# L copied from PSUM ahead of the masked product, and a score factor moved into q's norm weights, in a two-layer diffusion trunk

## Chip, core and metric

The kernel runs on one core of a Trainium2 chip, as one program. The metric is the device time in microseconds (us), of which three runs are shown below; smaller is better.

## What is computed

Two layers of a hybrid trunk over 640 tokens (512 latent, 128 context) with 1024 features, in float32. The first layer pairs MLA attention with retention, the second pairs differential attention (4 heads, two score maps of 64 features each) with a bidirectional RWKV-7 scan (8 heads of 64). Each layer ends in a gated convolutional FFN. What the change touches lies in the second layer:

```python
# differential attention, scale = 64 ** -0.5 = 0.125
q = rms_norm(dq, qn); k = rms_norm(dk, kn)
s = einsum('bqhcd,bkhcd->bchqk', q, k) * scale
p = softmax(s); w = p[:, 0] - lam * p[:, 1]; o = w @ v
# RWKV-7, one token at a time
state = state * w_t - (state @ kk_t) (kk_t * a_t)^T + v_t k_t^T
y_t = state @ r_t
```

## The kernel before

**Stages.** The program runs layer 0, then the FFN, then the input products of layer 1 (`odd_in`, `rwkv_in`), then the scan (`rwkv`, about 1045 to 1505 us of the span), then the output products and the second FFN. In the scan two streams are woven by hand: the main stream is the RWKV scan, the side stream (`side_mix`) first makes the differential q, k and v (`odd_qkv`) and then runs the differential attention (`diff_attn`). `BG` says how many steps of the side stream go into each part of the scan, and matrix products of the side stream are issued behind a main product of `LAG` = 4 events before. The final order of each engine's queue is made by the framework's scheduler when the program is built, from a timeline of its own; on the chip each engine works through its queue in that order.

**The scan.** It works on five groups g, each a block of 128 tokens forward and one backward. For each group there are three jobs: `pre(g)` makes the matrices of a block, `lb` and `lc` solve a small triangular system from the matrix L, and `steps(g)` carries the state over the two half blocks. They are staggered: with `steps(g)` run `pre(g+2)` and `lb(g+1)`, `lc(g+1)`.

**L.** In `rw_pre`, for each direction and each half block q, eight products (lines 1858 and 1859) fill the PSUM banks `sa` and `sb`, one bank each; the pool that these banks come from has two buffers in the scan. Then for s = 0 (`sa`) and s = 1 (`sb`) four instructions follow: VectorE multiplies the bank by the mask `mk` into `st[s]` (line 1863, 128x512, tile `hq`), ScalarE copies the left half of the rows into `L` (line 1864), GpSimd copies the right half into `rb` (line 1865), and ScalarE puts `kr` into the rows of `st[s]` that are now free (line 1866). That is 40 pairs of `sa` or `sb` in all. When both directions are done, `rw_leaf_a` sends L to DRAM and back (`ld<-L`, `LI<-ld`, lines 1884 and 1887); `rw_leaf_b` solves with 31 pairs of VectorE operations (lines 1901 and 1902), which read L above the diagonal only; `xd` goes to DRAM and back; `rw_leaf_c` makes `X11h` on ScalarE (line 1929) and writes `zb`, which `steps` needs.

**The scores.** In `diff_attn`, `s1` runs 40 times (4 heads, 5 query tiles, 2 maps): products into the one score buffer `sc` (line 1442), a row maximum with the sign turned (line 1445, VectorE), that maximum times 0.125 (line 1446, VectorE), and the exponential with that bias and the factor 0.125 (line 1448, ScalarE, tile `p`), which frees `sc` for the next one.

**q's norm weights.** `odd_qkv` multiplies q by its 64 weights `dqn`, which lie in the constant tile `rt` (line 1288, GpSimd).

Of the kernel before, what the change touches and what calls it, by code (L numbers as in the profile page):

```python
# [13 lines left out]
OP = mybir.AluOpType  # L14
# [90 lines left out]
def _consts3():  # L105
    """Head sums land in rows 32 p + i; the selectors bring rows 32 p + i and 32 p + 2 + i back to half i of tile p."""
    out = np.zeros((128, C3LEN), np.float32)
    st = out[:, C3OFF["st64"][0]:]
    st[:64, 0] = 1.0
    st[64:, 1] = 1.0  # L110
    st[:, 32:34] = 1.0 / 128
    sel = out[:, C3OFF["sel"][0]:].reshape(128, 4, 2, 64)
    for p in range(4):
        for i in range(4):
            sel[32 * p + i, p, i % 2] = 1.0
    return out
# [92 lines left out]

"""How the streams of the layers are woven: background steps in each part of the scan, spans of layer 0."""  # L210
BG = (89, 24, 102, 0, 22, 72, 0)
# [5 lines left out]
class Side:  # L217
    """A background stream: its matrix products are issued behind the main streams' product of LAG events before."""

# [21 lines left out]
def weave(bg, rate, *parts):  # L241
    """Advance several emission streams together; each (generator, begin, end) spreads evenly over [begin, end]."""
    ev = []
    for i, (g, b, e) in enumerate(parts):
        n = NSTEP[g.__name__]
        for k in range(n):
            ev.append((b + (e - b) * k / n, i))
    ev.sort()
    for _, i in ev:
        n0 = len(bg.traced()) if bg is not None else 0  # L250
        next(parts[i][0], None)
        if bg is not None:
            bg.mark(n0)
            bg.acc += rate / len(ev)
            while bg.acc >= 1:
                bg.acc -= 1
                bg.step()
    for g, _, _ in parts:
        for _ in g:
            pass  # L260


class Trunk:
# [116 lines left out]
    def setup_late(self):  # L380
        """The loads that nothing needs before the first products."""
        nc, a = self.nc, self.a
        self.rt = self.cp.tile([128, RLEN], F32, name="rt")
        for t, src in ((self.rt, bass.AP(tensor=a["row"].tensor, offset=a["row"].offset, ap=[[0, 128], [1, RLEN]])), (self.ct, a["cst"])):
            i = nc.sync.dma_start(t, src)
            self.tc.add_manual_dep(i.ins, self.fetched.ins.name, mybir.DependencyInfo(mybir.DependencyClass.NoSync, mybir.DependencyReason.DATA),
                                   reason="later")
        self.sel = self.cp.tile([128, 4, 128], F32R, name="sel")
        sel = self.W("sel", 512)
        nc.sync.dma_start(sel, a["cst3"][:, 64:])  # L390
        nc.gpsimd.tensor_copy(self.sel.rearrange("p a f -> p (a f)"), sel)
# [164 lines left out]
    def ada_half(self, c0):  # L556
        """Eight chunks of layer 0's modulation, from pieces that the queue brings in this order."""
        nc = self.nc
# [29 lines left out]
    def norm_mod(self, side):  # L588
        """Layer 0: rstd and x * rstd do not wait for the modulation."""
        nc = self.nc  # L590
# [25 lines left out]
    def norm_begin(self, l, which, pool):  # L616
        """Open the next norm: every final x[k] is scaled by the modulation and split at once, its rstd is applied after the
        matrix product; two more columns carry the shifts through it."""
        nc = self.nc
# [18 lines left out]
    def norm_end(self, us, rb):  # L638
        """Close the norm: the first three products run while the rstd is being worked out."""
        nc = self.nc  # L640
# [16 lines left out]
    def fm_norm(self, h, u, rb, ps=None):  # L657
        """One output tile of the normalised product, into the padded columns of u."""
        nc = self.nc
# [103 lines left out]
    def head_sums(self, sqs, stat, mmt, tile):  # L763
        """Per-head sums of four tiles of squares: [tokens, (token tile, tile, half)]."""
        nc = self.nc
# [15 lines left out]
    def head_rows(self, r, mmt, tile):  # L781
        """The [tokens, (token tile, tile, half)] columns as rows of hi and lo parts."""
        nc = self.nc
# [15 lines left out]
    def head_bcast(self, rows, p, mmt):  # L799
        """Tile p of the rows, spread over the features of its two heads."""  # L800
        mm = mmt()
        for b, e in ((192, 512), (512, 832)):
            for i, r in enumerate(rows):
                self.nc.tensor.matmul(mm[:, b:e], self.sel[:, p], r[:, b - 192:e - 192], start=i == 0, stop=i == len(rows) - 1)
        return mm[:, 192:832]

# [1 line left out]
    def even_jobs(self):  # L808
# [126 lines left out]
    def mla_cached(self, kr, ccs, D):  # L935
        """Keys and values of the cache, before the first products."""
        nc, a = self.nc, self.a
# [38 lines left out]
    def mla_rows(self, src, dst, tt, g, gain, D, tr):  # L976
        """Four heads of 128 tokens, turned to rows of features."""
        nc = self.nc
# [281 lines left out]

# [1 line left out]
    def odd_jobs(self):  # L1262
# [3 lines left out]
    def odd_qkv(self, D):  # L1266
        """Differential q, k, v from the stored h: one 256-column group at a time, its post-processing one group behind."""
        nc, a = self.nc, self.a
        with self.pool("qk", 1, "left") as qp, self.psum("qps", 2) as qps, self.psum("qtr") as qtr:
            def tile(s, w, bufs, dt=F32):  # L1270
                return qp.tile([128, w], dt, name=self.nm(s), tag=s, bufs=bufs)

            rope = qp.tile([128, 2, 4, 64], F32, name="ropd")
            nc.scalar.dma_start(rope.rearrange("p a t d -> p (a t d)"), a["ropd"])
# [92 lines left out]
    def odd_out(self, D):  # L1367
        """The differential half of w_out covers the end of the RWKV half."""
        nc = self.nc
# [38 lines left out]
    def diff_attn(self, D, ap, scp, trp):  # L1408
        nc, a = self.nc, self.a
        nlam = self.diff_lam(ap)  # L1410
        scale = 64 ** -0.5

# [22 lines left out]
        def s1(q, k, qt, so):  # L1435
            n = 768 if qt < 4 else 128
            pr = []
            for c in range(2):
# [6 lines left out]
                nc.vector.tensor_reduce(mx, sc[:, :n], axis=AX.X, op=OP.max, negate=True)  # L1445
                nc.vector.tensor_scalar(mx, mx, scale, None, op0=OP.mult)
                p = ap.tile([128, 768], F32, name=self.nm("p"), tag="p", bufs=4)[:, :n]
                nc.scalar.activation(p, sc[:, :n], AF.Exp, bias=mx, scale=scale, accum_out=sm)
                pr.append((p, sm))
# [291 lines left out]
    def rwkv_out(self, D, rp, o):  # L1741
        """D["u"] holds gate * gain and gate * v."""
        nc = self.nc
# [42 lines left out]
    def rw_pre(self, F, f, d, tt, L, hs, ex):  # L1786
# [52 lines left out]
        for q in range(2):  # L1839
# [21 lines left out]
            for s, rw, ps in ((0, lo, sa), (1, hi, sb)):  # L1861
                yield
                nc.vector.tensor_tensor(st[s], ps.rearrange("p (a c) -> p a c", a=4), mk, op=OP.mult)
                nc.scalar.copy(L[rw, sl, :], st[s][rw, :, 0:64])
                nc.gpsimd.tensor_copy(rb[rw], st[s][rw, :, 64:128])
# [248 lines left out]
```

## Time and profile before

| | |
|---|---|
| device time, three runs | 2068.95, 2071.0, 2071.74 us (median 2071.0) |
| span of the profiled execution, first to last instruction | 2059.5 us |
| device time around the span, against the three runs | 9.5 to 12.2 us |
| PE busy in the span | 1952.7 us (95%) |
| DVE, ACT, POOL busy | 1253.8, 887.3, 186.5 us |

The profile is one execution; its own device time isn't listed beside its span, so the three runs stand for it. PE is TensorE's products, PEld its weight loads, DVE is VectorE, ACT ScalarE, POOL GpSimd, SPq the queue of SyncE that issues transfers. In a row `out<-in` names what an instruction writes and reads, `x40` how often; after it stand times in us or, for the mean of one, in ns. `<-X` names what ended an engine's idle time.

### The profile page before, as it was taken

How to read it: one execution, taken by the hardware profiler on the slowest of the kernel's cores; microseconds unless marked ns; L12 is line 12 of the kernel's file. 1: busy time of each engine (PE TensorE's matmuls, PEld its weight loads, DVE VectorE, ACT ScalarE, POOL GpSimd, SP SyncE). 2: the span in 40 equal slices, each digit the busy share in tenths (PEclk: the TensorE clock that was granted, in tenths of full speed). 3: DMA queues.
4: the chain of work that ended last, by engine and by line, in shares of the span. 5: the costliest groups of instructions: out<-in, count | busy, mean ns of one | idle time of the engine just before them, and what ended most of it. 6: DMA issues, size and time to landing. Idle time of an engine off the chain costs nothing.

```text
span 2059.5 us, 36275 instructions
## 1 busy us (share of the span) xinstructions
PE 1952.7 (95%) x14376; PEld 1765.7 (86%) x14376; DVE 1253.8 (61%) x2752; ACT 887.3 (43%) x1680; POOL 186.5 (9%) x365
## 2 busy tenths in 40 slices
PE   6999999999999999999989897898779999999999
PEld 3998565999899899999978676777679999999999
DVE  6554657556456465577436856877667764656555
ACT  4433344334244243456333334667534542524343
POOL 1001000000000000000024332332110000000000
PEclk9999999999999999999989998979989999999999
DMA  8237344234543512143264554454453212122221
GB/s 323 67 109 242 105 134 163 89 104 147 181 153 116 192 62 83 60 151 104 83 207 100 109 161 120 100 116 96 100 200 106 77 58 92 60 85 67 77 63 71
DMA packets 190676, 243.60 MB, mean 118 GB/s; under 512 B 90730, under 2 KB 132970, under 8 KB 190508
## 3 DMA queue, kind: packets, MB, share of 16 engines
q1 hardware_dynamic: 184880, 225.87, 35.7%
q0 software_dynamic: 3904, 13.37, 2.2%
q8 instruction: 113, 1.85, 0.4%
q10 hardware_dynamic: 1724, 2.06, 0.3%
q14 instruction: 55, 0.45, 0.1%
HBM read 202.05 MB, written 39.21 MB: 117 GB/s over the span
## 4 chain that ended last, share of the span: by engine, by line
PE 81%; DVE 7%; DMA 6%; ACT 3%; issue 2%; POOL 1%; SPq 0%; ACTq 0%; DVEq 0%; POOLq 0%
PE mm L470 59%; PE qkv L1325 2%; PE ada L541 2%; PE rv L913 1%; PE pv L1130 1%; PE mm L1097 1%; DMA dk<-pt 1%; PE ptr L1120 1%; PE sc L1442 1%; DVE X L1902 1%; DVE tmp L1901 1%; DMA xd<-X 1%; DMA mq<-tr 1%; DMA raw<-ada 1%; PE mm L1098 1%
## 5 line engine op out<-in xcount | busy, mean ns | idle before, releaser
L414 ACT CAST hi<-raw 128x1024 fp32r<-128x1024 f32 (+4 forms) x212 | 195.9, 925 | 574.1 <-PE mm L470 528.6
L470 PE MATMUL mm<-hhi,hi 128*128 128x322 f32 x1648 | 381.0, 312 | 0.0
L470 PE MATMUL mm<-hlo,hi 128*128 128x322 f32 x1648 | 380.3, 311 | 0.0
L470 PE MATMUL mm<-hhi,lo 128*128 128x322 f32 x1648 | 380.1, 311 | 0.0
L470 PEld LDWEIGHTS mm<-hhi,hi 128*128 128x128 f32 x1648 | 278.3, 189 | 8.7 <-issue 6.7
L470 PEld LDWEIGHTS mm<-hlo,hi 128*128 128x128 f32 x1648 | 279.5, 190 | 0.0
L470 PEld LDWEIGHTS mm<-hhi,lo 128*128 128x128 f32 x1648 | 278.6, 189 | 0.0
L415 DVE TENSOR_TENSOR lo<-raw,hi 128x1024 fp32r<-128x1024 f32 (+4 forms) x212 | 226.1, 1067 | 58.7 <-ACT hi L414 36.0
L672 DVE SCALAR_TENSOR_TENSOR x<-mm,ada,x 128x512 f32<-128x512 f32 (+1 forms) x176 | 88.7, 545 | 176.1 <-PE mm L470 175.9
L470 PE MATMUL mm<-ahi,hi 128*128 128x320 f32 x704 | 161.7, 311 | 0.0
L470 PE MATMUL mm<-ahi,lo 128*128 128x320 f32 x704 | 160.7, 309 | 0.0
L470 PE MATMUL mm<-alo,hi 128*128 128x320 f32 x704 | 160.3, 309 | 0.0
L663 DVE COPY shv<-mm 128x2 f32<-128x2 f32 x103 | 16.3, 159 | 207.9 <-PE mm L470 207.9
L470 PEld LDWEIGHTS mm<-ahi,hi 128*128 128x128 f32 x704 | 117.1, 188 | 12.0 <-ACT hi L414 10.1
L1325 PE MATMUL qkv<-w,x 128*128 128x256 f32 x480 | 118.9, 402 | 0.1
L470 PEld LDWEIGHTS mm<-ahi,lo 128*128 128x128 f32 x704 | 117.8, 188 | 0.0
L470 PEld LDWEIGHTS mm<-alo,hi 128*128 128x128 f32 x704 | 117.6, 188 | 0.0
L666 ACT ACTIVATE u<-u,shv 128x128 f32<-128x128 f32 (+1 forms) x176 | 90.3, 557 | 48.8 <-DVE u L665 47.0
L734 DVE SCALAR_TENSOR_TENSOR ac<-u,vt,ac 128x642 f32<-128x642 f32 x88 | 78.0, 887 | 52.5 <-ACT ac L732 52.3
L1325 PEld LDWEIGHTS qkv<-w,x 128*128 128x128 f32 x480 | 94.0, 201 | 17.0 <-issue 1.7
L732 ACT ACTIVATE ac<-u,vt 128x642 f32<-128x642 f32 x88 | 81.3, 925 | 2.8
L665 DVE TENSOR_TENSOR u<-mm,rb 128x128 f32<-128x128 f32 (+1 forms) x176 | 77.3, 481 | 2.5 <-ACT rb L650 2.5
(419 smaller groups left out, 3351.3 us busy)
## 6 DMA issues: line engine op xcount, KB each, us to landing
raw<-ada SPq DMA_DIRECT2D x96, 512.0 KB, 4.6
raw<-up SPq DMA_DIRECT2D x88, 512.0 KB, 3.5
raw<-down SPq DMA_DIRECT2D x32, 384.0 KB, 3.1
raw<-down SPq DMA_DIRECT2D x32, 320.0 KB, 2.8
fs<-df SPq DMA_DIRECT2D x10, 832.0 KB, 5.2
raw<-wb_fm SPq DMA_DIRECT2D x15, 512.0 KB, 3.5
w<-wb_tm SPq DMA_DIRECT2D x12, 512.0 KB, 4.5
raw<-wa_fm SPq DMA_DIRECT2D x11, 512.0 KB, 4.3
```

The lines of the kernel that those rows point to most:

```text
L414: nc.scalar.copy(hi, t)
L415: nc.vector.tensor_tensor(lo, t, hi.bitcast(F32), op=OP.subtract)
L470: nc.tensor.matmul(ps[:, c0 + b:c0 + e], wt[:, ws], at[:, b:e], start=first and j == 0, stop=last and j == 2)
L541: nc.tensor.matmul(ps[32 * j:32 * j + 32, :], self.cs[:, k, :], pieces[j // 2][:, (j % 2) * 512:(j % 2) * 512 + 512], start=k == 0, stop=k ...
L665: nc.vector.tensor_tensor(u[:, o], ps[:, s], rb[:, s], op=OP.mult)
L666: nc.scalar.activation(u[:, o], u[:, o], AF.Identity, bias=sh[:, c:c + 1])
L672: nc.vector.scalar_tensor_tensor(x[:, s], ps[:, s], self.ada_v(l, part, m, c), x[:, s], op0=OP.mult, op1=OP.add)
L732: nc.scalar.activation(ac, u[:, 1:643], AF.Identity, scale=cv[:, 1, f:f + 1], bias=self.vec(f"cb{l}", f))
L734: nc.vector.scalar_tensor_tensor(ac, u[:, 0:642], cv[:, 0, f:f + 1], ac, op0=OP.mult, op1=OP.add)
L913: nc.tensor.matmul(ps[:, :272], at[:, ts], wt[:, k * 272:k * 272 + 272], start=n == 0, stop=n == 23)
L1097: nc.tensor.matmul(sc[:, 0:512], q, kT[:, 0:4], start=True, stop=True)
L1325: nc.tensor.matmul(ps, h[k][:, t * 128:t * 128 + 128], w[k // 4][:, k % 4 * 256:k % 4 * 256 + 256], start=k == 0, stop=k == 7)
```

## The change

`L` is copied from the PSUM bank itself, and this copy now stands ahead of the masked product in the program; the masked product reads the same bank after it. The mask is no longer applied to L, of which only the part above the diagonal is read. The factor 0.125 is multiplied once into the 64 weights `dqn` at the start of `odd_qkv`; the 40 multiplications of the maximum and the factor in the exponential are gone. The rest of the diff takes away comments.

```diff
@@ odd_qkv
+            nc.vector.tensor_scalar(self.row("dqn"), self.row("dqn"), 0.125, None, op0=OP.mult)
             rope = qp.tile([128, 2, 4, 64], F32, name="ropd")
@@ diff_attn
         nlam = self.diff_lam(ap)
-        scale = 64 ** -0.5
...
                 nc.vector.tensor_reduce(mx, sc[:, :n], axis=AX.X, op=OP.max, negate=True)
-                nc.vector.tensor_scalar(mx, mx, scale, None, op0=OP.mult)
                 p = ap.tile([128, 768], F32, name=self.nm("p"), tag="p", bufs=4)[:, :n]
-                nc.scalar.activation(p, sc[:, :n], AF.Exp, bias=mx, scale=scale, accum_out=sm)
+                nc.scalar.activation(p, sc[:, :n], AF.Exp, bias=mx, accum_out=sm)
@@ rw_pre
             for s, rw, ps in ((0, lo, sa), (1, hi, sb)):
                 yield
-                nc.vector.tensor_tensor(st[s], ps.rearrange("p (a c) -> p a c", a=4), mk, op=OP.mult)
-                nc.scalar.copy(L[rw, sl, :], st[s][rw, :, 0:64])
+                pv = ps.rearrange("p (a c) -> p a c", a=4)
+                nc.scalar.copy(L[rw, sl, :], pv[rw, :, 0:64])
+                nc.vector.tensor_tensor(st[s], pv, mk, op=OP.mult)
                 nc.gpsimd.tensor_copy(rb[rw], st[s][rw, :, 64:128])
                 nc.scalar.copy(st[s][rw], kr[rw])
```

## Rows read from the trace of the kernel before

**Rows 1.** The page, part 1: busy time, share of the span, instructions.

```profile
PE 1952.7 (95%) x14376; PEld 1765.7 (86%) x14376; DVE 1253.8 (61%) x2752; ACT 887.3 (43%) x1680; POOL 186.5 (9%) x365
```

**Rows 2.** Windows: stretch, length, PE, PEld, DVE, ACT, POOL busy, clock, DMA, GB/s.

```profile
1230.00:1505.00 275.00, 231.99 (x2915) 190.24 (x2915) 194.59 (x625) 166.03 (x427) 72.35 (x125) 0.86 0.49 119
...
1298.00:1343.00 45.00, 39.07 (x428) 31.86 (x428) 41.76 (x147) 28.97 (x78) 16.38 (x28) 0.92 0.38 101
1369.00:1413.00 44.00, 40.81 (x497) 33.45 (x492) 40.26 (x142) 29.29 (x77) 14.97 (x26) 0.93 0.31 81
1434.00:1470.00 36.00, 29.86 (x398) 24.51 (x394) 30.40 (x126) 18.36 (x49) 7.09 (x13) 0.87 0.48 120
```

**Rows 3.** The chain that ended last, 1421 to 1475: start, us, what.

```profile
1421.70 0.42 ACT X11h L1929
...
1425.49 0.41 ACT L L1864
...
1429.42 5.03 DMA LI<-ld
...
1470.38 4.52 DMA xd<-X
```

**Rows 4.** Timeline, first operation of a leaf solve: start, us, instruction, [idle before].

```profile
1298.64 0.19 DVE L1901 TENSOR_TENSOR tmp<-LI,X 128x31 f32<-128x31 f32 x1 [2.95 <-DMA LI<-ld]
```

**Rows 5.** Lines by form, 1030 to 1520: busy us, mean ns, idle before, releaser.

```profile
L1863 DVE TENSOR_TENSOR hq<-sa,c 128x512 f32<-128x512 f32 x20 | 13.7, 684 | 7.6 <-PE sa L1858 7.3 <-DMA w<-wb_tm 0.2
...
L1864 ACT COPY L<-hq 64x256 f32<-64x256 f32 x40 | 16.1, 403 | 32.9 <-DVE hq L1863 32.2
...
L1982 ACT ACTIVATE SV<-pa 64x256 f32<-64x256 f32 x40 | 15.1, 377 | 6.0 <-PE pa L1980 5.5
...
L1446 DVE TENSOR_SCALAR mx<-mx 128x1 f32<-128x1 f32 x40 | 5.8, 146 | 0.4
```

**Rows 6.** Windows, the instructions of line 1446 alone: stretch, length, DVE busy, clock.

```profile
1298.00:1343.00 45.00, 1.00 (x7) 0.92 0.38 101
1369.00:1413.00 44.00, 0.86 (x6) 0.93 0.31 81
1434.00:1470.00 36.00, 1.16 (x8) 0.87 0.48 120
```

**Rows 7.** Timeline, one maximum: reduce, scale, exponential.

```profile
1317.01 0.94 DVE L1445 TENSOR_REDUCE mx<-sc 128x1 f32<-128x768 f32 x1
...
1318.75 0.14 DVE L1446 TENSOR_SCALAR mx<-mx 128x1 f32<-128x1 f32 x1
...
1318.92 0.90 ACT L1448 ACTIVATE p<-sc,mx 128x768 f32<-128x768 f32 x1 [0.39 <-DVE mx L1446]
```

**Rows 8.** Waits, 1030 to 1520: us in total, times, longest.

```profile
ACT p L1448 <- DVE mx L1446: 18.5, 13, 3.9
...
ACT wT L1474 <- DVE ao L1473: 10.3, 8, 2.8
```

**Rows 9.** Timeline: VectorE reads a PSUM tile that ScalarE has just read.

```profile
1041.34 0.82 DVE L1537 TENSOR_TENSOR v<-v,mm 128x640 f32<-128x640 f32 x1 [0.69 <-ACT g L1536]
```

**Rows 10.** Line 1863, who waited for it: us, times.

```profile
  PEld kt L1873: 3.8, 1
...
  PEld sa L1858: 0.8, 2
  PEld lf L1933: 0.2, 1
```

**Rows 11.** Timeline: masked products and their L copies, first and last of eight.

```profile
1320.08 0.68 DVE L1863 TENSOR_TENSOR hq<-sa,c 128x512 f32<-128x512 f32 x1
...
1321.50 0.41 ACT L1864 COPY L<-hq 64x256 f32<-64x256 f32 x1
...
1395.59 0.68 DVE L1863 TENSOR_TENSOR hq<-sb,c 128x512 f32<-128x512 f32 x1
...
1397.00 0.40 ACT L1864 COPY L<-hq 64x256 f32<-64x256 f32 x1
```

## What the change does to the time, predicted before it ran

> **What bounds the kernel now.** I read part 1 of the page first: PE is busy for 95% of the span [rows 1], so over the whole program only time that PE loses can be won back. Then the windows: the one stretch in which PE has room and in which all the edits lie is the scan, and in its second part, 1230 to 1505, PE is busy for 232.0 of 275.0 us, at a granted clock of 0.86 [rows 2]. What sets the pace there is a loop over the groups: the matrix L of a group is finished, goes to DRAM and back, is solved by 31 pairs of dependent VectorE operations, and the solved block then feeds the state steps. The chain that ended last shows the end of one turn: the copies of L wait on ScalarE behind `X11h`, the last one runs at 1425.49, the transfer back lands at 1434.45, and the solve ends where its result leaves at 1470.38 [rows 3]. The first of the last three solves shows the same start: VectorE stood idle for 2.95 us until `LI<-ld` had landed [rows 4]. The solve itself is bound by VectorE: in the three stretches in which the last three solves run, VectorE is busy for 41.76 of 45, 40.26 of 44 and 30.40 of 36 us [rows 2], since the attention's and the next group's operations stand between those of the solve. So two things count here: how early L is ready, and how much else VectorE has to do, or stands still for, while it solves.
>
> **The score factor.** 40 multiplications of a 128x1 column go, 146 ns each, 5.8 us of VectorE in all [rows 5]. In the three solve stretches there are 7, 6 and 8 of them, which take 1.00 + 0.86 + 1.16 = 3.0 us [rows 6], and VectorE's time is the path there: I take 3.0 us off. The other 19 take 2.8 us; they lie between reduction and exponential, on the attention's own chain, which shares the path with the scan: half of it, 1.4 us off. The lower bound of the gain is zero, where the scan's chain and not the attention's ends last at each place. The upper bound comes from the waits: the scheduler has put other operations between reduction and multiplication, in the example shown the reduction ends at 1317.95 and the multiplication runs only at 1318.75, with the exponential right behind it at 1318.92 [rows 7]. After the change the exponential can follow the reduction. ScalarE waited for this multiplication 13 times, 18.5 us in all [rows 8]; those waits hold the reductions too, so 18.5 us is more than can be won. The exponential without its factor has the same length. What takes the place of this wait is the score buffer: the next products can't start before the exponential has read it.
>
> The one new multiplication, 128x64, is bounded below by the 0.146 us of the column and above by the 0.684 us of the 128x512 product [rows 5]. It stands at the head of the side stream, and VectorE has all of the first group's products ahead of q's norm to hide it; without that cover it costs its own 0.15 to 0.7 us, once. Zero.
>
> **L ahead of the masked product.** Before, a bank was multiplied (0.684 us) and the copy waited for that: ScalarE stood idle for 32.2 us before these copies [rows 5]. Now the copy needs the products alone, so L can be ready 0.7 us earlier. It counts in the two turns of the loop where the solve waited for L's transfer [rows 3, 4]: 1.4 us off. On top of that stands ScalarE's queue. In the last turn the copies stood behind `X11h`, which itself waited for a transfer until 1421.70, and the last one ran at 1425.49 [rows 3]. If the scheduler, which now sees the copies ready before `X11h`, puts them ahead of it, up to 3.8 us come off; if it doesn't, nothing. I take half, 1.9 us, since some of the four copies of that batch can pass and some can't. The copy itself reads PSUM instead of SBUF; the nearest row is another 64x256 copy out of PSUM at 377 ns against 403 [rows 5], 1 us over 40, on an engine with room: zero.
>
> Now the price. Two reads of one PSUM tile by two engines don't run side by side in this program. VectorE's read of `mm` on line 1537 stood idle until ScalarE's read of it on line 1536 had ended [rows 9], though neither uses what the other writes, and all 8 times that ScalarE waited at line 1474 it was for VectorE's copy out of the same tile [rows 8]. So the masked product gets a wait that it didn't have: it starts at least one copy, 0.38 us, after the products' end, 0.4 us with the signal. The Trainium skill says why a program has to be built so (PSUM — Partial Sum Buffer, section "PSUM bank collisions raise a hardware error"): two engines may not touch the same bank in the same 32 partitions at once, two reads included; the trace agrees, with an idle time before each such second read in [rows 8, 9], and if the rule did not hold here the sum below would be 1.6 us lower and the slower rival would fall.
>
> What waits behind the product: the bank, held 0.4 us longer, out of a pool of two. Others waited for the product's bank 4 times [rows 10]; 4 times 0.4 is 1.6 us, which I add in full. GpSimd's copy into `rb` and ScalarE's copy of `kr` come 0.4 us later; they are needed by `steps` two groups on, a solve of 36 us [rows 3] away, and cost nothing while that cover stands, 0.4 us a group without it. On VectorE everything queued behind the product waits with it; the lower bound of that is zero, if the scheduler puts other ready work ahead of it, and the upper bound is the second rival.
>
> **The sum.** -3.0 - 1.4 - 1.4 - 1.9 + 1.6 = -6.1 us. Against the profiled span of 2059.5 us that is 2053.4 us; the median of the three runs stands 11.5 us above that span, and I take this distance as unchanged: 2064.9, so **2065 us**. About 0.2%, 4 us, is what a measurement of this kernel can tell from no change; the three runs lie 2.8 us apart.
>
> **The rivals.**
>
> *It is absorbed.* The attention and the scan share the engines, and the time that a shorter maximum frees goes into waits for the score buffer or for PE, while the copies stay behind `X11h`. For it: most solves aren't waiting for L, and PE is at 84% in this stretch. Against it: VectorE at 84 to 93% in the solves. The terms left are -1.4 for L and +1.6 for the bank, with a part of the 3.0: 2070 us.
>
> *VectorE stands still for ScalarE.* The masked product now sits in VectorE's queue behind a copy in ScalarE's queue, and the solve's operations stand behind the product. If the queues keep their order, the product starts when the copy, which starts where it started before, is done. In the solve stretches there are eight such products. The first ran at 1320.08 while its copy ran at 1321.50; at 0.38 us for the copy and its signal it would start at 1321.88, 1.8 us late. The last goes from 1395.59 to 1397.38, again 1.8 us [rows 11]. The same subtraction over the eight gives 12.6 us. It speaks for it that ScalarE holds state copies and exponentials in those places; against it, that the scheduler knows of the wait and can fill it. With all other gains kept but the queue's 1.9 us the sum is -3.0 - 1.4 - 1.4 + 1.6 + 12.6 = +8.4, so 2079 us. It decides from 6 us on: at that the gains are gone.
>
> *More comes off.* The copies pass `X11h` in full (3.8 instead of 1.9), and the exponentials win half of the 18.5 us instead of 1.4: -3.0 - 9.2 - 1.4 - 3.8 + 1.6 = -15.8, 2055 us.
>
> That the edits don't do what they say I leave out: all 40 multiplications have gone from the text, and nothing reads L below the diagonal.
>
> **How the numbers follow.** The forecast has 0.40, its spread reaching from 2061 to 2069, so a quarter of it lies within 0.2% of 2071; absorbed 0.25, nearly all within; VectorE's stalls 0.22, all slower; more 0.13, all faster. Faster: 0.30 + 0.13 + 0.04 = 0.47; within: 0.10 + 0.20 = 0.30; slower: 0.22 + 0.01 = 0.23. The range goes from 2056, which leaves out the lower part of the fourth case, to 2080, which leaves out the upper part of the third, about 2 in 10 together. The forecast's own range is 2061 to 2069.
>
> **What would show it.** Right: line 1446 is gone and exponentials wait for line 1445 alone; the last `L` copy of each group ends sooner behind its products, and `LI<-ld` lands sooner; from the end of the input products to the first product of the output the scan is some 6 us shorter, with the stretches before and behind it as they were. The price shows as idle time of VectorE before line 1863 that ScalarE's copy ended: some 16 us over 40 are the 0.4 us of the copy, far more is the second rival. I am wrong if the solves are no shorter while VectorE does less, if the copies still stand behind `X11h`, or if the time moves in stretches that hold none of the edits.

## The result, and the profile after

| | before | after |
|---|---|---|
| device time, median (lowest to highest) | 2071.37 us (2068.95 to 2073.06) | 2095.11 us (2086.95 to 2101.09) |
| ratio to before | | 1.0112, 95% interval [1.0076, 1.0148] |
| span of the profiled execution | 2059.5 us | 2094.5 us |

The change makes the kernel 24 us slower; forecast was 2065, and the time lies above the range too. The profiled execution of after has its own time, 2096.56, so 2.1 us lie around the span and not 9.5 to 12.2. The execution of before that was profiled was thus one of the quick ones, about 2061 us; over all batches, on four chips, the runs of before lie between 2055 and 2087. Of the 35 us between the two spans, some 11 are that.

Part 1 of the page of after, for [rows 1]:

```profile
PE 1981.0 (95%) x14376; PEld 1784.7 (85%) x14376; DVE 1254.0 (60%) x2713; ACT 886.2 (42%) x1680; POOL 188.2 (9%) x365
```

VectorE has lost its 39 instructions (40 go, one comes), TensorE does the same 14376 in 28 us more. The windows show where, and that the granted clock is lower there (1.00 is the 2.4 GHz level, 0.50 the 1.2 GHz level): length, PE, PEld, DVE, ACT, POOL busy, granted clock, DMA share, GB/s, for the part before the scan and the part of the scan from the last q, k, v product to the last product of a state step. Before:

```profile
0.00:1045.70 1045.70, 1009.79 (x6827) 901.20 (x6828) 606.07 (x1235) 431.72 (x741) 40.24 (x110) 1.00 0.41 135
1231.00:1504.10 273.10, 230.99 (x2911) 189.63 (x2911) 193.94 (x623) 164.63 (x423) 71.35 (x123) 0.86 0.49 117
```

After:

```profile
0.00:1057.60 1057.60, 1020.16 (x6827) 909.24 (x6828) 606.64 (x1236) 431.91 (x741) 39.94 (x110) 0.99 0.41 133
1245.10:1537.80 292.70, 249.94 (x2912) 202.19 (x2911) 191.02 (x577) 164.93 (x426) 68.59 (x121) 0.81 0.44 106
```

The 11.9 us ahead of the scan aren't the change's. `fill_ok`, a kernel of the study below that has neither edit and in which nothing ahead of the scan differs from before, takes nearly as long there in its profiled execution. In its windows:

```profile
0.00:1056.70 1056.70, 1020.01 (x6828) 908.60 (x6829) 606.36 (x1235) 431.84 (x741) 39.84 (x110) 0.99 0.42 134
```

What remains is the attention part of the scan, 292.7 us against 273.1, at a granted clock of 0.81 against 0.86. The loop turns more slowly there; a turn is the time from the first operation of a leaf solve to that of the next. The first operation of the third solve of before is in [rows 4], at 1298.64. Its timeline shows the last operation of that solve, and the first and last of the next ones:

```profile
1342.12 0.17 DVE L1902 TENSOR_TENSOR X<-X,tmp 128x16 f32<-128x16 f32 x1
...
1366.61 0.17 DVE L1901 TENSOR_TENSOR tmp<-LI,X 128x31 f32<-128x31 f32 x1
...
1411.84 0.17 DVE L1902 TENSOR_TENSOR X<-X,tmp 128x16 f32<-128x16 f32 x1
...
1434.57 0.19 DVE L1901 TENSOR_TENSOR tmp<-LI,X 128x31 f32<-128x31 f32 x1 [0.84 <-DMA LI<-ld]
```

and that of after shows the same:

```profile
1312.03 0.19 DVE L1901 TENSOR_TENSOR tmp<-LI,X 128x31 f32<-128x31 f32 x1 [2.39 <-DMA LI<-ld]
...
1360.00 0.17 DVE L1902 TENSOR_TENSOR X<-X,tmp 128x16 f32<-128x16 f32 x1
...
1383.74 0.19 DVE L1901 TENSOR_TENSOR tmp<-LI,X 128x31 f32<-128x31 f32 x1 [2.33 <-DMA LI<-ld]
...
1420.10 0.17 DVE L1902 TENSOR_TENSOR X<-X,tmp 128x16 f32<-128x16 f32 x1
...
1464.44 0.19 DVE L1901 TENSOR_TENSOR tmp<-LI,X 128x31 f32<-128x31 f32 x1 [1.87 <-DMA LI<-ld]
```

Two turns of 68.0 us have become 71.7 and 80.7, and VectorE stands waiting for L's transfer at the start of each of the three solves (before: 2.95 us [rows 4], none, 0.84). The solves themselves aren't what grew: the two took 43.7 and 45.4 us, and now take 48.1 and 36.5. From the end of the fourth solve to the start of the fifth it was 22.6 us and is 44.2. TensorE runs 445 products in that stretch, against 264 before. Among them is `wp`, which opens the preparation of the second direction's L, and which in before had run by then. So the next L comes later.

The edit did what it says, all the same. Lines by form of after, for [rows 5] (line 1863 is now the copy, 1864 the product):

```profile
L1864 DVE TENSOR_TENSOR hq<-sa,c 128x512 f32<-128x512 f32 x20 | 13.7, 687 | 6.5 <-ACT L L1863 5.9 <-DMA w<-wb_tm 0.4
L1864 DVE TENSOR_TENSOR hq<-sb,c 128x512 f32<-128x512 f32 x20 | 13.7, 687 | 14.0 <-ACT L L1863 14.0
L1863 ACT COPY L<-sb 64x256 f32<-64x256 f32 x20 | 7.4, 368 | 9.1 <-PE sb L1858 8.9
```

The copies follow the products, at 368 ns; VectorE's product waits for the copy, 5.9 + 14.0 = 19.9 us in all. That is the price that the prediction named, and nearly its size (16). It invites the story that this wait is the loss. The experiments say that it isn't.

### The profile page after: what moved, and what is told of

Read it like the earlier page. It is cut to its first block, busy times and chain, and to the rows that moved or that the text cites. A ratio compares the mean times of both kernels' runs of the same rounds, so it can differ in the third digit from the quotient of the medians.

```text
span 2094.5 us, 36213 instructions
## 1 busy us (share of the span) xinstructions
PE 1981.0 (95%) x14376; PEld 1784.7 (85%) x14376; DVE 1254.0 (60%) x2713; ACT 886.2 (42%) x1680; POOL 188.2 (9%) x365
```

## The experiments

All ratios are to the kernel before, run beside each on the same chip, in five rounds.

| kernel | L edit | score edit | queue order | us | ratio, interval |
|---|---|---|---|---|---|
| l_only | yes | | its own | 2089.3 | 1.0104 [1.0060, 1.0149] |
| s_only | | yes | its own | 2074.25 | 1.0027 [1.0002, 1.0052] |
| s_late | | yes, elsewhere | its own | 2076.15 | 1.0041 [1.0014, 1.0067] |
| hoist_only | | times 1.0 | as before | 2071.17 | 1.0009 [0.9983, 1.0036] |
| l_pin | yes | | before's | 2065.07 | 0.9982 [0.9959, 1.0006] |
| order_only | | | l_only's | 2093.51 | 1.0106 [1.0073, 1.0138] |
| s_pin | | yes | before's | 2069.77 | 1.0000 [0.9975, 1.0024] |
| all_pin | yes | yes | before's | 2073.96 | 1.0008 [0.9982, 1.0034] |
| fill_before | | | before's, fillers | 2057.58 | 0.9934 [0.9907, 0.9961] |
| fill_order | | | l_only's, fillers | 2083.89 | 1.0050 [1.0024, 1.0076] |
| fill_l | yes | | before's, fillers | 2056.12 | 0.9920 [0.9893, 0.9948] |
| regroup | | | l_only's, mended (VectorE) | 2099.61 | 1.0146 [1.0111, 1.0182] |
| split_2nd | | | before's, spoiled (VectorE) | 2070.97 | 1.0008 [0.9984, 1.0031] |
| fill_ok | | | before's, fillers | 2052.6 | 0.9918 [0.9888, 0.9949] |
| fill_l_ok | yes | | before's, fillers | 2057.76 | 0.9941 [0.9916, 0.9965] |
| pe_regroup | | | l_only's, mended (TensorE) | 2090.85 | 1.0098 [1.0063, 1.0133] |
| both_regroup | | | l_only's, both mended | 2098.12 | 1.0122 [1.0090, 1.0154] |
| hyb_t3 | | | before's, then l_only's | 2087.45 | 1.0076 [1.0049, 1.0103] |

**Which edit.** `l_only` is the third hunk of the change alone, `s_only` the first two. `s_late` puts the scaled weights into a tile of their own, `hoist_only` is before with a multiplication that changes nothing:

```diff
 s_late, in odd_qkv
+            gq = qp.tile([128, 64], F32, name="gq")
+            nc.vector.tensor_scalar(gq, self.row("dqn"), 0.125, None, op0=OP.mult)
...
+                gain = gq if name == "q" else self.row(gain)
 hoist_only, in odd_qkv
+            nc.vector.tensor_scalar(self.row("dqn"), self.row("dqn"), 1.0, None, op0=OP.mult)
```

> Only the L edit: L is copied from PSUM ahead of the masked product; the score factor stays where it was. If the masked product's wait for ScalarE's copy is the cost (theory A, the second rival of the prediction), this alone is slower by more than 8 us, most of the 24 us, the prefix up to the scan takes what it took before (scan starts at 1046 us, give or take 1), and all of the loss lies between 1046 us and the end of the scan. If the early multiplication of the weights is the cost (theory B: the scheduler put it into layer 0, at position 67 of VectorE's queue, and the profiled run lost 12 us before the scan), this alone is within 5 us of before. If any change of the queues' order costs, whatever it is (theory C), this and the next two are all slower by 5 us or more.

> Only the score edit, as in the change: 0.125 multiplied into the weights in place, no multiplication of the maximum, no factor in the exponential; L as before. Theory A: 0 to 6 us faster than before. Theory B: 10 to 15 us slower, all of it before 400 us of the span, where the profiled run of the change lost 12 us. Theory C: slower by 5 us or more, in the scan.

> The score edit with the multiplied weights in a tile of their own that exists only from the scan on, so that the multiplication can't be queued earlier; L as before. Theory A: 0 to 6 us faster than before, as s_only. Theory B: faster than s_only by 10 to 15 us, and the stretch before the scan as before. Theory C: slower than before by 5 us or more.

> The kernel before with one VectorE instruction more, in the place where the change has it: the weights multiplied in place by 1.0; all else as before. Theory A: within 3 us of before. Theory B: 10 to 15 us slower, before 400 us of the span. Theory C: it depends on how far the queues change; if the order of the scan's queues stays, within 3 us.

The L edit carries the loss by itself; the score edit costs a quarter of a per cent where it should have gained, and the new multiplication costs nothing that can be measured. Both edits also changed something that the diff doesn't show: the scheduler laid the queues of the scan anew. Against before, `l_only` has another instruction in 612 of VectorE's 2752 places, 1387 of TensorE's 12004 and 328 of ScalarE's 1591, all from the scan on; `hoist_only`, which costs nothing that can be measured, has the scan's order unchanged. The change itself has yet another order than `l_only`.

**The edit or the order.** Each engine's queue can be written down and forced on another build by edges of order, which add no semaphore; before with its own order forced on it is the same program, instruction for instruction and wait for wait. So the edit and the order can be swapped:

```diff
+    for name, text in _ORDER.items():      # each engine's queue, as places in the traced program
...
+            if prev is not None:
+                tc.add_manual_dep(cur, prev.name, dep, reason="pin")   # NoSync: order only
 l_pin, order_only and all_pin leave the L copies free on ScalarE
-                nc.scalar.copy(L[rw, sl, :], ...)
+                _FREE.append(nc.scalar.copy(L[rw, sl, :], ...).ins.name)
```

> The L edit alone (copy from PSUM ahead of the masked product), but with every engine's queue pinned to the order that the kernel before has; only the L copies themselves are free to find their place on ScalarE (they move by one to four places). Before is taken as 2069 to 2071 us, and the L edit with the order that the compiler's scheduler gave it took 2089, 1.0104 of before. Theory 'dependency' (the masked product waits for ScalarE's copy, VectorE and the bank are held, all else is a consequence): the queue order does not matter, 2083 to 2092 us, a ratio of 1.006 to 1.011. Theory 'order' (the scheduler wove the scan anew around the edit, and the new weave leaves TensorE waiting more): 2062 to 2073 us, a ratio of 0.996 to 1.002, with the attention part of the scan back at about 273 us.

> The kernel before, neither edit made (L is still copied from the masked product), but with every engine's queue pinned to the order that the scheduler gave the L edit alone; only the L copies are free on ScalarE. Theory 'dependency': nothing waits that did not wait before, 2067 to 2075 us, a ratio of 0.999 to 1.003. Theory 'order': the new weave costs what the L edit cost, 2083 to 2093 us, a ratio of 1.006 to 1.011, with the attention part of the scan at about 290 us and the granted clock there lower.

> The score edit alone (no multiplication of the maxima, 0.125 in q's norm weights), every queue pinned to the order of the kernel before with the 40 multiplications taken out. With the scheduler's own order this edit took 2074, 1.0027 of before. Theory 'order': that small loss was the reshuffle too, so pinned it shows the 3 to 5 us that the multiplications were forecast to cost: 2064 to 2069 us, a ratio of 0.997 to 0.9995. Theory 'dependency' says nothing of this edit; if the multiplications were hidden and the loss is in the edit itself, 2071 to 2076 us.

> Both edits, that is the change itself, with every queue pinned to the order of the kernel before (the 40 multiplications taken out, the L copies free on ScalarE). The change took 2095, 1.0112 of before. Theory 'order': at a fixed order the change is worth what the prediction summed, about 6 us less than before: 2060 to 2069 us, a ratio of 0.995 to 0.999. Theory 'dependency': 2080 to 2090 us, a ratio of 1.005 to 1.010, as the waits of VectorE for ScalarE's copy stay.

The first two decide it for the L edit. The old code in `l_only`'s order takes 1.0106 of before, the L edit in the old order 0.9982. For the change itself the pair is after and all_pin: the same two edits, 1.0112 in the scheduler's order and 1.0008 in the old one, with intervals that don't touch. The old code wasn't run in the change's own order. The wait for the copy doesn't make the loss by itself. In `l_pin` VectorE waits for ScalarE's copy longer than it does in the changed kernel, 17.0 + 13.7 = 30.7 us, and its twelve times show no loss; lines by form:

```profile
L1865 DVE TENSOR_TENSOR hq<-sa,c 128x512 f32<-128x512 f32 x20 | 13.7, 687 | 17.7 <-ACT L L1864 17.0 <-DMA w<-wb_tm 0.6
L1865 DVE TENSOR_TENSOR hq<-sb,c 128x512 f32<-128x512 f32 x20 | 13.7, 687 | 13.7 <-ACT L L1864 13.7
```

In `order_only`, 22 us slower than before by its median, it never waits for ScalarE there, and for TensorE as long as in before; the same view of order_only, and of before for `sb` (7.3 us for `sa` are in [rows 5]):

```profile
L1863 DVE TENSOR_TENSOR hq<-sa,c 128x512 f32<-128x512 f32 x20 | 13.7, 683 | 6.4 <-PE sa L1858 6.4
L1863 DVE TENSOR_TENSOR hq<-sb,c 128x512 f32<-128x512 f32 x20 | 13.6, 682 | 4.6 <-PE sb L1859 4.6
```

```profile
L1863 DVE TENSOR_TENSOR hq<-sb,c 128x512 f32<-128x512 f32 x20 | 13.7, 684 | 4.3 <-PE sb L1859 4.2
```

One profiled execution would have told another story. That of `l_pin` was the slowest of its twelve (2079.19), and its attention part took 282.2 us, where its expectation under the order theory was about 273:

```profile
1240.50:1522.70 282.20, 243.90 (x2911) 198.84 (x2911) 194.45 (x623) 163.77 (x424) 71.31 (x123) 0.81 0.47 114
```

Its fourth turn took 80.2 us, as long as in after, and that of hoist_only, in before's order without either edit, 76.2. In both the solve was the long part (54.5 and 54.4 us). What tells the orders apart is the time from a solve's end to the next solve's start. In the profiled executions with before's order it lies between 21.0 and 24.3 us behind the third solve and between 21.8 and 26.1 behind the fourth. In `l_only` it is 42.2 and 30.7 us, in order_only 43.5 and 32.1, in after 23.6 and 44.2.

The score edit's small loss is likely the order too: pinned it is 1.0000, though the intervals of s_only and s_pin overlap. No gain of it can be seen, where its expectation had one. In all_pin the two edits together show none either, 1.0008.

**Is it the clock?** Windows of order_only: the attention part of its scan, and inside it the stretch where TensorE has little to do and two of the four stretches behind that:

```profile
1239.40:1541.80 302.40, 257.50 (x2911) 207.01 (x2911) 195.63 (x623) 165.36 (x425) 73.17 (x127) 0.77 0.45 109
...
1400.40:1407.40 7.00, 3.37 (x39) 2.59 (x39) 7.00 (x21) 3.72 (x9) 2.00 (x1) 0.80 0.22 47
1407.40:1414.40 7.00, 7.00 (x32) 5.34 (x32) 6.24 (x23) 2.59 (x5) 0.39 (x1) 0.50 0.01 4
...
1428.40:1435.40 7.00, 7.00 (x47) 5.26 (x47) 2.58 (x13) 4.42 (x12) 0.39 (x1) 0.50 0.00 0
```

TensorE worked for 3.37 of 7 us, and then ran at the 1.2 GHz level (0.50) from 1407 to 1435, busy throughout with 32 to 47 products in 7 us; from 1393 to 1400, at a clock of 0.93, it did 92. Eight products into `sb` take 1.16 us at a clock of 1.00 (before) and 2.07 us at 0.50 (after), by the timelines:

```profile
1320.01 1.16 PE L1859 MATMUL sb<-kr,kb 64*128 64x128 f32 x8
```

```profile
1410.72 2.07 PE L1858 MATMUL sb<-kr,kb 64*128 64x128 f32 x8
```

The length of the attention part times (1 - clock) is 273.1 x 0.14 = 38 us in before and 302.4 x 0.23 = 70 us in order_only. Taken off, 235 and 233 us remain, as if the order cost nothing but clock. To test that, fillers, products that nothing reads, went into TensorE's queue at the scan's idle gaps, with every order as it was. In fill_before, fill_order and fill_l they also disturb the sums of `yp` in the other half of their bank, so what these three compute in y isn't the reference's; instructions and waits are the same.

```diff
 fill_before, fill_order, fill_l: ahead of the products that TensorE waits for
+                f = nc.tensor.transpose(self.yps[d][:, 256:384], self.ident, self.ident)
 fill_ok, fill_l_ok
+                f = nc.tensor.matmul(self.yps[d][:, 256:512], self.sel[:, 0], self.sel[:, 0:2],
+                                     start=False, stop=True, skip_group_check=True)
```

> The kernel before with its own queue order pinned, plus 164 transposes of 128x128 on TensorE whose results nothing reads (into the unused half of a PSUM bank), put ahead of the 43 places in the scan where the trace of before shows TensorE idle for over 0.3 us, and sized by 0.26 us each to about 85% of each idle gap. All else is as in before (before is 2071). Theory 'clock': what an order costs is TensorE's granted clock, which falls to half after it has idled, so the idle microseconds themselves are cheap and the halved stretches behind them dear; filled, the scan's clock loss (about 54 us of clock-weighted time in the profile of before) shrinks by a third or more and the kernel gets faster, 2035 to 2060 us. Theory 'waits': the clock is a by-product, the chain through VectorE and ScalarE sets the scan's end; the fillers can only delay it, 2071 to 2085 us.

> The kernel before in the queue order that the scheduler gave the L edit (order_only, 2093.5 us, 1.0106 of before), plus 179 such transposes at the 43 idle gaps of order_only's own trace. Theory 'clock': with TensorE kept busy the two orders come together, since span less clock loss is the same for both within 5 us (1995.7 for both): 2035 to 2068 us, at most 12 us from fill_before. Theory 'waits': the order keeps its cost, 2090 to 2105 us, 20 us or more from fill_before.

> The L edit alone in the queue order of before (l_pin, 2065.1 us, 0.9982 of before), plus 166 such transposes at the 45 idle gaps of l_pin's trace. Theory 'clock': 2030 to 2055 us, within 8 us of fill_before. Theory 'waits': 2065 to 2080 us.

Filling pays in either order: 0.66% in before's, and from 1.0106 to 1.0050 in the new one, where the two intervals barely overlap. But fill_order stays 26 us behind fill_before, where the clock theory allowed 12. So the clock isn't all of the cost, and the subtraction above misled. A slow TensorE may have covered waits that show once it is fast; no run shows that by itself. Nor did the fillers bring the two clocks together. Windows of fill_before:

```profile
1229.10:1489.80 260.70, 234.18 (x3033) 191.58 (x3032) 193.91 (x623) 163.88 (x423) 71.33 (x123) 0.92 0.52 123
```

and of fill_order:

```profile
1228.40:1525.60 297.20, 258.31 (x3039) 208.34 (x3039) 194.87 (x623) 164.66 (x425) 73.08 (x127) 0.85 0.45 111
```

Less the clock's part by the same rough estimate, 260.7 x 0.92 = 240 and 297.2 x 0.85 = 253 us remain: 13 of the 37 us between these two stretches. The profiled execution of fill_before was its quickest, so the two lie 36 us apart and their medians 26. What the order does is seen best in these two. TensorE's timeline in the third turn of fill_before, which begins at 1293.77:

```profile
1313.66 1.16 PE L1860 MATMUL sa<-kr,kb 64*128 64x128 f32 x8
...
1315.17 1.16 PE L1861 MATMUL sb<-kr,kb 64*128 64x128 f32 x8
...
1325.00 1.12 PE L1793 MATMUL wp<-wup,wx 65*128 65x512 f32 x2
```

and of fill_order, where it begins at 1290.18:

```profile
1318.29 0.93 PE L1861 MATMUL sb<-kr,kb 64*128 64x128 f32 x6 [0.18 <-DVE mx L1446]
1319.44 0.73 PE L1442 MATMUL sc<-ak,aq 128*128 128x512 f32 x2 [0.21 <-ACT p L1448]
...
1320.33 0.49 PE L1861 MATMUL sb<-kr,kb 64*128 64x128 f32 x2
...
1329.23 0.68 PE L1875 MATMUL kt<-ident,kb 64*128 64x64 f32 x8 [0.54 <-DVE hq L1865]
...
1333.30 0.69 PE L1965 MATMUL yp<-ident 128*128 128x128 f32 x2 [1.84 <-ACT ys L2020]
...
1338.20 1.22 PE L1793 MATMUL wp<-wup,wx 65*128 65x512 f32 x1
```

The first direction's products into `sb` stand in one piece in before's order. In the new one a score product stands among them and waits for an exponential, so that `sb`, the masked product, its bank and the next pair wait for the softmax. That cut is a small part of the delay: some 1 us lies between the two pieces, and `sb` begins 21.4 us into the turn in the one and 28.1 in the other. `wp`, which opens the second direction, comes 31.2 us into the turn in the one and 48.0 in the other. (The 1.84 us are the fillers' own, a wait for the bank's reader.) The turn's end, the first operation of the next solve, fill_before:

```profile
1358.46 0.19 DVE L1903 TENSOR_TENSOR tmp<-LI,X 128x31 f32<-128x31 f32 x1 [1.65 <-DMA LI<-ld]
```

fill_order:

```profile
1374.49 0.19 DVE L1903 TENSOR_TENSOR tmp<-LI,X 128x31 f32<-128x31 f32 x1 [6.65 <-DMA LI<-ld]
```

64.7 us against 84.3, and VectorE stands idle for 6.65 us because L comes late.

**Where in the order.** Two features of the new order could be mended alone or put into the old one alone: the masked products stand further apart in VectorE's queue, and five groups of products are cut in TensorE's.

```diff
 regroup: two groups of four masked products, places behind the first in VectorE's queue
-    +13 +27 +34  and  +12 +15 +24
+    +4  +11 +16  and  +3  +9  +19
 split_2nd: the same two groups in before's order
-    +4  +11 +16  and  +3  +9  +19
+    +13 +14 +17  and  +12 +13 +19
 pe_regroup: five groups of four products in TensorE's queue
-    sb sb sb sc sc sc sc sb   (and four like it)
+    sb sb sb sb sc sc sc sc
 both_regroup: regroup and pe_regroup
 hyb_t3: before's order up to the fourth leaf solve, l_only's from there on
```

> The kernel before in the scheduler's order for the L edit (order_only, 2093.5 us, 1.0106 of before), with one thing put back: in the last two turns of the scan in which the first direction's preparation runs beside the leaf solve, the four masked products stand in VectorE's queue at the distances they have in before (4, 7, 5 and 3, 6, 10 instructions apart in place of 13, 14, 7 and 12, 3, 9); the first of the four stays where it is, and so does all else. Theory 'spread' (the new order is dear because solve and softmax instructions stand between the masked products, which hold the scan's two PSUM banks): 2076 to 2087 us, a ratio of 1.003 to 1.0075. Theory 'elsewhere' (the loss sits in other parts of the order, for instance TensorE's queue or where the preparation starts): 2089 to 2097 us, 1.0085 to 1.012.

> The converse: the kernel before in its own order, with the second masked product moved back in VectorE's queue in the same two places, to stand 13 and 12 instructions behind the first as in the L edit's order (4 and 3 in before); the third and fourth are moved only as far as they must be to stay behind it. Theory 'spread': sb's bank is freed some 3 us later, twice, and the turn follows: 2074 to 2082 us, 1.002 to 1.005. Theory 'elsewhere': no difference that can be measured, 0.998 to 1.002.

> The kernel before in the scheduler's order for the L edit (order_only 2093.5 us, 1.0106), with TensorE's queue mended in one respect: in the attention part of the scan five groups of four products into sa or sb stand there cut in two, with 18 attention products between their parts (score products that wait for the softmax to free their bank); in before no group is cut there. The tails are pulled up behind their heads; all else, VectorE's queue among it, stays as in order_only. Theory 'cut groups': the masked products and all that hang on them come 2 to 5 us sooner in each of the last two turns: 2078 to 2089 us, a ratio of 1.004 to 1.0085. Theory 'whole weave' (no single place; the new order has attention work ahead of the scan's in many places of several queues, so mending one moves the wait to the next): 2089 to 2100 us, 1.009 to 1.0145.

> The two repairs together: order_only with TensorE's five cut groups made whole and the four masked products of the two places at the distances of before in VectorE's queue (regroup, which did the second alone, took 1.0146: VectorE then stood waiting for the cut sb products). Theory 'cut groups': each repair needs the other, so together they give most of the loss back: 2072 to 2084 us, a ratio of 1.001 to 1.0065. Theory 'whole weave': 2086 to 2100 us, 1.0075 to 1.0145.

> The kernel before in its own order up to the first instruction of the fourth leaf solve (about 1366 us in its trace), and from there on in the scheduler's order for the L edit. If the order's cost is spread over the turns, as the traces of fill_order against fill_before say (19.6 us in the third turn, 14.5 in the fourth, so some four tenths of it in the part that is now new), the kernel takes 2076 to 2084 us, a ratio of 1.003 to 1.0065. If it sits in the third turn alone, or is set off there and only carried on, 2067 to 2074 us, 0.9985 to 1.002. If it sits in the last turn and the tail alone, 2087 to 2096 us, 1.008 to 1.012.

The theories of a single place fell one after the other: regroup gives nothing back (1.0146, with an interval that overlaps order_only's), split_2nd costs nothing that can be measured, whole groups in TensorE's queue give nothing back that can be measured, and both repairs together don't either. hyb_t3, with only the fourth turn and what follows in the new order, takes 1.0076. That lies between the range for a cost spread over the turns (to 1.0065) and that for the last turn alone (from 1.008), and its interval reaches into both; the third turn alone is excluded. But the splice is an order of its own: its fourth turn took 89.7 us, against 79.0 and 83.8 in l_only and order_only. So it doesn't say how the cost is shared among the turns. What the traces show is where the time appears: between one solve's end and the next one's start, where the next L is made. That the cause is the whole weave, attention work ahead of the scan's in many places, fits all of these runs but was shown by none; which places carry the cost is open. Also open is why the scheduler chose this order. That the copy's 0.4 us in its own timeline tipped it is likely, but wasn't tried.

**A kernel that beats both.** The gaps of fill_before were filled by half, since its transposes take less time than assumed. So with twice as many fillers, of a kind that leaves `yp` alone:

> As fill_before, with the filler products changed: a 128x128 by 128x256 product each that accumulates into the unused half of the bank (start not set, so that the sums of yp in the other half stay what they are), and 342 of them in place of 164, since the trace of fill_before shows 20 of its transposes in 2.40 us, 0.12 us each where 0.26 had been assumed. Theory 'clock' (fill_before took 0.9934 of before, and its scan lost 28 us of clock in place of 54): 2040 to 2058 us, a ratio of 0.985 to 0.9935. Theory 'waits' (the fillers now stand ahead of products that could have run): 2058 to 2075 us.

> The L edit in the order of before (l_pin, 0.9982 of before) with 339 such fillers at the idle gaps of l_pin's trace. With the fillers of the first kind this took 0.9920. Theory 'clock': 2038 to 2056 us, a ratio of 0.984 to 0.992, level with fill_ok within 6 us. Theory 'waits': 2057 to 2075 us.

Windows of fill_ok:

```profile
1238.40:1502.60 264.20, 248.64 (x3165) 207.31 (x3165) 193.66 (x623) 164.15 (x424) 72.03 (x123) 0.94 0.52 121
```

The scan's attention part runs at a clock of 0.94 in place of 0.86, and the kernel is 0.8% faster than before and, by the two ratios, some 2% faster than the change. Twice the fillers give little more than the first lot (0.9918 against 0.9934, intervals that overlap), though the clock rose from 0.92 to 0.94. The L edit adds nothing to it that can be measured.

## Why the prediction was wrong, step by step

**The step that failed** is the one on which the sum was built without saying so: that the edits act on the queues as they stood. The text let the scheduler move the L copies, and only for the better ("puts them ahead of it", half of 3.8 us), or fill the masked product's wait. In fact the scheduler laid the whole scan anew. In the L edit's order that is worth +22 us with the old code (order_only), more than three times the whole sum; for the change it is the 1.0112 of after against the 1.0008 of all_pin. In the terms of the prediction, the path from a solve's end to the next L was to change by the terms for L alone, and to get shorter; in the fourth turn it grew from 22.6 to 44.2 us, while the solve shrank.

**The bank's price**, a start 0.4 us later, 16 us over 40: right in place and nearly in size, 19.9 us; but it costs nothing that can be measured. l_pin waits 30.7 us and isn't slower; its interval excludes the rival's 12.6 us, and the 1.6 of the sum would not show in it. In all_pin it waits 32.4 us, at 1.0008.

**The rival "VectorE stands still for ScalarE"** came nearest in time, 2079, but that is luck: its mechanism is refuted by the same run. l_pin makes its condition true, queues that keep their order, but for the L copies, which may move by one to four places.

**L sooner and past `X11h`** (-1.4 and -1.9, with +1.6 for the bank, so 0.9992 of before): l_pin's 0.9982 [0.9959, 1.0006] agrees, and can't tell it from nothing. The passing itself didn't come: in the last group of l_pin two L copies, though free, still follow an `X11h` copy each (1438.84 after 1437.64, 1440.16 after 1439.21), and in after all four follow the two of 1441.38.

**The score factor** (-3.0 and -1.4): s_pin is 1.0000 [0.9975, 1.0024]. The forecast 0.9979 lies just inside, so s_pin doesn't refute it; the sum of both edits, 0.9971, lies just outside all_pin's interval. "VectorE's time is the path there" is thus not borne out, and which of the two edits' gains is missing stays open. The exponentials' wait for the maximum, 18.5 us in 13 waits in before [rows 8], now ends at the reduction (line 1445). With the order held it shrank, and no time came of it; waits of all_pin:

```profile
ACT p L1447 <- DVE mx L1445: 10.7, 7, 3.4
```

In after, in the new order, it grew:

```profile
ACT p L1447 <- DVE mx L1445: 25.8, 16, 4.2
```

**The distance to the profile**: 11.5 us "around the span" were some 2 us of overhead (2.1 in after); the rest says that the profiled execution was a quick one. It did no harm, as the sum was a difference, but it hid that one kernel's executions lie 1.5% apart.

**The signs.** The 40 multiplications are gone and the copies follow their products, as forecast. Of the signs named for being wrong, that of the solves gave no warning: they took 43.7, 45.4 and 35.8 us before and 48.1, 36.5 and 32.6 after, shorter in sum, while the turns grew. The copies still follow `X11h` copies, but with 5 us between (1441.38 and 1447.51), and two of the last four wait for TensorE's products. A scan that is 20 us longer at the same work was in none of the cases.

## What to carry to other kernels

Where a scheduler orders the queues at build time, an edit of half a microsecond is also a new draw of the order of everything around it, and in a woven stretch that draw can outweigh the edit. Compare the queues of the two builds before explaining a wait, and cost an edit with the old order pinned; if pinned it is neutral and free it is slower, keep the order and not the verdict on the edit. A long wait that an edit adds proves nothing until a run has the wait without the loss, or the loss without the wait. One profiled execution doesn't price an edit either: with the scan's queues unchanged, one turn took 68.0 us in one execution and 76.2 in another.

## What the runs showed of the hardware that was not expected

The executions of one kernel spread with TensorE's granted clock: before lies between 2055 and 2087 us, with a mean clock of 0.968 in the quickest and 0.955 in the slowest. Profiled executions with the order of before show 1.00 or 0.99 ahead of the scan, for 1045.7 (before) or 1056.7 us (fill_ok) of the same work. In the scan, with the same queues, the fourth turn took 68.0 us at a clock of 0.89 (before) and 76.2 at 0.75 (hoist_only).

Keeping TensorE busy with products that nothing reads pays here: 342 of them, at 0.13 us each in a row (26 in 3.38 us), make the kernel faster by 0.8% (0.9918), and the scan's attention part has a clock of 0.94 in place of 0.86.

Transposes into the unused half of a PSUM bank, placed between two parts of a sum in the other half, changed the sum: y moved by more than half its size (0.57). With products that don't set start, in the same gaps, the sum held. The Trainium skill has a rule that fits (PSUM — Partial Sum Buffer, section "The four PSUM rules"): the first product of a group clears the marks that say "written" for a whole bank, in the groups of 32 partitions that it writes, so that the next part of another sum there overwrites in place of adding. The runs agree, though kind of product and flag were changed together, so that the flag alone isn't shown.
